# Attention on one Trainium2 core: the product of the second weight block with V written as seven smaller products in every inner period, and two partial outputs added by the Pool engine

## The chip, the cores and the metric

The kernel runs on one core of one Trainium2 chip. The metric is the device time of one execution in microseconds (us). The core has a matrix engine (TensorE; PE in the profile, its weight loads PEld), a vector engine (DVE), a scalar engine (ACT), the Pool engine (POOL) and a queue engine (SP) that only issues transfers. Each engine takes its instructions strictly in the order in which they were written, and an instruction that waits holds all that stand behind it on its engine.

## The reference

```python
# q, k, v: (8, 2048, 512) float32
d_k = q.shape[-1]
scores = np.matmul(q, k.transpose(0, 2, 1)) / np.sqrt(d_k)
attn_weights = special.softmax(scores, axis=-1).astype(np.float32)
return np.matmul(attn_weights, v)
```

## The kernel before

Both matrix products of attention are computed by Winograd's form of Strassen's method: the two operands are cut into 2 x 2 blocks, and seven block products replace eight, at the price of sums of blocks. Operands are fp16, and products gather in fp32 banks of PSUM, the memory that TensorE writes. Softmax needs no maximum here: `exp` of the scaled scores is taken at once, and the row sums come out of the second product through a column of ones that stands beside V; outputs are multiplied by their reciprocal (`rate`, L469).

**Periods and slots.** There are 8 batches, and each is cut into four periods of 28 slots: 32 periods, numbered g = 0 to 31; a period's place in its batch is g % 4, called qt. One slot holds one product of Q and K for the scores that are needed two periods later (`Group.product`, two matmuls of 512 columns at L332) and, between them, the products of weights and V that a text places there ("a6@20" is product 6 of the row block a at slot 20). Lists of words of the same form (`SUMS`, one for each qt, with some in `SUMS_AT` for single g) say at which slot which sum of blocks is given to DVE. So the order of each engine is written out by hand, and the engines run free within it, held by semaphores alone.

**Weights times V.** A period computes two row blocks, a and b, each as seven products with 256 columns (`Pair.product`, L437: eight matmuls for each product, as the contraction runs over eight pieces, `NJ`). The sums of weight blocks come from `p_sums` (L385 to L388; words S, N, L), those of V blocks from `v_sums` (L222 to L225; words v01 to v14). The weights of a pair of periods lie in the tiles `left` (two of them) and `right`.

**Inner products.** In the periods g = 1 to 29 some of these seven products are taken for a and b together and are again written as seven smaller ones of 128 columns (`fine`, L586: four matmuls each, so 28 instead of 16). Its stages 1 to 4 are the words s1..s4 for product 1 (called x), t1..t4 for product 2 (y) and u1..u4 for product 5 (z). Which of them are inner is said by `INNERS`, by qt: `("xz", "xyz", "xyz", "xz")`. So in qt 0 and 3 product 2 is still the plain one (words a2 and b2). An inner product needs four sums of weight blocks on DVE (`a_sums`, L555 to L558; words x1..x4, y1..y4, z1..z4, written to the tiles `si1`, `si2`, `si4` and in place), and once in a batch four sums of V blocks (`vi_sums`, L256 to L259; words X, Y, Z). Between its stages ACT copies a 256-column half of a bank (L601) and two 128-column parts into `ci` (L604, L609), and DVE adds the latter to a bank (L610, L614).

**Outputs.** ACT multiplies a bank of 256 columns by the reciprocal row sum into an output tile `o` (`scaled`, L446), and DVE adds a second bank to it (`final`, L449). The output quarter C11 is the sum of product 1 and product 2. Where product 2 is inner, C11 is made by `scaled` from x and `final` from y (`after2`). Where it is not, ACT copies x to a fresh bank (L529), product 2 gathers on top of it, and `scaled` writes the sum. There are seven `o` tiles. SP stores each of them (`store`, L456, 128 KB).

**Loads.** POOL issues the loads of the next batch (`load`, L127, for Q and K into two `stage` tiles; `load_v`, L214, for V), SP issues the transposing transfers from `stage` (`dma_transpose`, L153) between its stores. A load waits for the transposing transfer that empties its `stage` tile; the transposing transfer waits for the load.

Of the kernel before, what the change touches and what calls it, by code (L numbers as in the profile page):

```python
# [12 lines left out]
def kernel(  # L13
# [47 lines left out]
    NP = B * NQT  # L61
    inv_sqrt_d = float(1.0 / np.sqrt(D))
# [5 lines left out]
    opool = ctx.enter_context(tc.tile_pool(name="opool", bufs=7))  # L68
# [35 lines left out]
    si = {n: const.tile([P, NI, P], F16, name=f"si{n}") for n in (1, 2, 4)}  # L104
    ui = {n: const.tile([P, NI, P + 2 if n == 1 else P], F16, name=f"ui{n}") for n in (1, 2, 4)}
    ti3 = const.tile([P, NI, P], F16, name="ti3")
# [109 lines left out]
    def v_sums(b, c):  # L216
        vh = vraw[b % 2]
        js = slice(c * NI, (c + 1) * NI)
# [14 lines left out]
    def t3_inner(b, s):  # L233
        if s == 1:
            return ti3[:]
        if b + 1 == B:
            return vi_blocks(b + 1)[s // 2][:, 0]
        return vu_blocks()[1] if s else vi_blocks(b)[1][:, 0]
# [5 lines left out]
    def vi_sums(b, s):  # L244
        if not ti:
            for n in (1, 2, 4):
                ti[n] = ipool.tile([P, 2, NI, P + 2 if n == 1 else P], F16, tag=f"t{n}", name=f"ti{n}")
            nc.gpsimd.memset(ti[1][:, 1, :, P:P + 1], 0.0)
        if s == 2:
            b11, b12, b21, b22 = vu_blocks()  # L250
            t1, t2, t4 = ui[1][:, :, 0:P], ui[2][:], ui[4][:]
        else:
# [9 lines left out]
    def new_p(sp):  # L262
        left = [ppool.tile([P, NJ, QH], F16, tag=f"left{s}", name=f"left{s}") for s in range(2)]
        right = ppool.tile([P, NJ, 2, QH], F16, tag="right", name="right")
        pts[sp] = (left, right)
# [4 lines left out]
    def plain_tile(kb, half, name):  # L270
# [8 lines left out]
        left, right = pts[0]  # L279
# [20 lines left out]
    class Group:  # L300
# [6 lines left out]
        def product(self, n):  # L307
# [6 lines left out]
            if n == 1:  # L314
                if self.sp not in pts:
                    new_p(self.sp)
                self.left, self.right = pts[self.sp]
# [52 lines left out]
    def p_sums(g, which, j0=0, j1=NJ):  # L370

        left, right = pts[g // 2]
# [27 lines left out]
    class Pair:  # L400
# [8 lines left out]
        def product(self, n, j0=0, j1=NJ):  # L409
            g = self.g  # L410
            left, right = pts[g // 2]
# [41 lines left out]
        def store(self, o, half, ds):  # L453
            b, sp = divmod(self.g // 2, NSP)
            n = (2 * sp + half) * NT + self.g % 2 * 2 + "ab".index(self.which)
            nc.sync.dma_start(out=out[b, n * P:(n + 1) * P, ds], in_=o)  # L456
# [43 lines left out]

    class Fine(Pair):
# [18 lines left out]
        def part(self):  # L520
# [6 lines left out]
            else:  # L527
                self.y = bank("pz")
                nc.scalar.copy(out=self.y[:, 0:H], in_=self.x[:, 0:H])  # L529

        def after2(self):
            if "y" in INNER(self.g):
# [19 lines left out]
    def a_sums(g, s):  # L552
        a11, a12, a21, a22 = a_blocks(g, s)
        return [
            lambda: add(si[1][:], a21, a22),  # L555
            lambda: sub(si[2][:], si[1][:], a11),
            lambda: sub(a21, a11, a21),
            lambda: sub(si[4][:], a12, si[2][:]),  # L558
        ]

    def fine(g, s, stage):
# [8 lines left out]
        else:  # L570
            b11, _, b21, b22 = (x[:, s] for x in vi_blocks(g // NQT))
            t1, t2, t4 = ti[1][:, s, :, 0:P + s], ti[2][:, s], ti[4][:, s]
        pa, pb = (pairs.setdefault((g, w), Fine(g, w)) for w in "ab")
        name = "xyz"[s]
        if stage == 1:
            for p in (pa, pb):
                setattr(p, name, bank("pz" if s else "px"))
        xa, xb = getattr(pa, name), getattr(pb, name)

        def product(n, dst):  # L580
            lhs, rhs = {
                1: (a11, b11), 2: (a12, b21), 3: (si[4], b22), 4: (a22, t4),
                5: (si[1], t1), 6: (si[2], t2), 7: (a21, t3_inner(g // NQT, s)),
# [14 lines left out]
        if stage == 1:  # L598
# [3 lines left out]
        elif stage == 2:  # L602
            product(6, xb[:, 0:P])
            nc.scalar.copy(out=ci[:, 0], in_=xb[:, 0:P])  # L604
            product(2, xa[:, 0:P])
        elif stage == 3:
            product(3, xa[:, P:P + W])
            product(7, xb[:, 0:P])
            nc.scalar.copy(out=ci[:, 1], in_=xb[:, 0:P])  # L609
            nc.vector.tensor_add(xa[:, P:H], xa[:, P:H], ci[:, 0])  # L610
            done(pa)
        else:
            product(4, xb[:, 0:P])
            nc.vector.tensor_add(xb[:, P:H], xb[:, P:H], ci[:, 1])  # L614
# [15 lines left out]
    def INNER(g):  # L630
        return "" if g == 0 or g >= NP - 2 else "xyz" if g % NQT in (1, 2) else "xz"

    INNERS = ("xz", "xyz", "xyz", "xz")

    def INNER(g):
        return "" if g == 0 or g >= NP - 2 else INNERS[g % NQT]

    def placed(text):
# [8 lines left out]
        "a7'@1 b7'@2 a4'@6 u1@8 b4'@9 u2@9 s1@12 u3@12 s2@13 u4@14 s3@15 a3@15 s4@16 b3@18 a6@20 "  # L647
        "a2@22 b6@24 b2@27",
        "a7'@1 b7'@3 a4'@5 u1@7 b4'@10 u2@10 s1@11 u3@12 s2@13 u4@14 s3@15 a3@16 s4@17 b3@18 "
        "a6@20 t1@21 t2@23 b6@24 t3@25 t4@27",  # L650
# [286 lines left out]
```

## Time and profile before

| | |
|---|---|
| median of three timed runs | 791.18 us (790.97 to 791.58) |
| the profiled execution, its own time | 792.15 us |
| its span, from the first instruction to the last | 790.4 us |
| PE busy in the span | 783.1 us, 99% |
| DVE busy | 690.1 us, 87% |
| ACT busy | 629.1 us, 80% |
| POOL busy | 71.8 us, 9% |
| granted TensorE clock | 0.999 of full speed |

The busy time of PE says that a matmul was under way, not that PE was at its peak: matmuls are pipelined, and one that lasts 273 ns starts 109 ns after the one ahead of it. On DVE and ACT too an instruction may begin before the one ahead of it has ended. POOL's busy time before is that of issuing loads, and of a few small instructions at the start.

### The profile page before, as it was taken

Reading aid. Unit: us, or ns where it says so; the run is one execution under the profiler, and the core shown is the slowest. Engines: PE = TensorE matmul, PEld = TensorE weight load, DVE = VectorE, ACT = ScalarE, POOL = GpSimd, SP = SyncE. Lnnn points to the kernel's source line nnn. Section 1 sums busy time; section 2 is a strip of 40 time slices with the busy share of each in tenths; the row PEclk is TensorE's granted clock in tenths of the full one; section 3 lists DMA queues with packets and bytes.
Section 4 is the critical chain, followed back from the end, with each engine's and each line's share of the span. In section 5 each row is a group of like instructions: output and inputs, shape, how many; then the busy total and the mean of one; then the engine's idle time right before and its main releaser. Section 6 shows DMA issues by size and latency. Waiting matters only on the chain.

```text
span 790.4 us, 17347 instructions
## 1 busy us (share of the span) xinstructions
PE 783.1 (99%) x6406; PEld 536.7 (68%) x6406; DVE 690.1 (87%) x1508; ACT 629.1 (80%) x1267; POOL 71.8 (9%) x108
## 2 busy tenths in 40 slices
PE   8999999999999999999999999999999999999998
PEld 5556666666666666666666676666676666666686
DVE  2789999979998899988999889997999979999774
ACT  4777888887888888888888888888888888888852
POOL 4011110101100110001100101001010011000000
PEclk9999999999999999999999999999999999999999
DMA  9989996899949999398994899768897799921122
GB/s 224 179 130 159 177 186 124 142 179 153 183 104 172 176 178 185 71 170 138 189 183 98 164 166 176 146 129 156 157 171 150 133 161 163 185 68 37 45 67 96
DMA packets 206453, 116.02 MB, mean 147 GB/s; under 512 B 124320, under 2 KB 205344, under 8 KB 206368
## 3 DMA queue, kind: packets, MB, share of 16 engines
q0 software_dynamic: 49648, 49.29, 43.2%
q1 hardware_dynamic: 156432, 65.30, 38.1%
q8 instruction: 50, 0.82, 0.4%
q14 instruction: 35, 0.29, 0.1%
q10 hardware_dynamic: 288, 0.33, 0.1%
HBM read 100.73 MB, written 33.55 MB: 170 GB/s over the span
## 4 chain that ended last, share of the span: by engine, by line
PE 98%; DMA 1%; ACT 1%; DVE 0%; SPq 0%; issue 0%; ACTq 0%
PE t L332 46%; PE t L437 33%; PE t L586 15%; PE t L275 2%; DMA first<-in_k_dram 1%; PE tr L163 1%; PE t L291 0%; PE tr L140 0%; ACT left L268 0%; ACT right L268 0%; SPq L134 0%; DVE kraw L166 0%; DVE cz L357 0%; ACT cz L348 0%; ACT kraw L142 0%
## 5 line engine op out<-in xcount | busy, mean ns | idle before, releaser
L332 PE MATMUL t<-qraw,kraw 128*128 128x512 f16 x728 | 200.7, 379 | 0.1
L446 ACT ACTIVATE o<-t,r 128x256 f32<-128x256 f32 x256 | 118.5, 477 | 69.1 <-PE t L437 34.6
L268 ACT ACTIVATE left<-t 128x512 f16<-128x512 f32 (+1 forms) x260 | 154.4, 599 | 17.8 <-PE t L332 10.0
L332 PE MATMUL t<-qs,ks 128*128 128x512 f16 x488 | 139.7, 378 | 0.2 <-DVE cz L357 0.2
L268 ACT ACTIVATE right<-cz 128x1024 f16<-128x1024 f32 x122 | 129.4, 1061 | 4.5 <-DVE cz L354 4.5
L437 PEld LDWEIGHTS <-s 128*128 128x128 f16 x1072 | 103.9, 97 | 38.3 <-DVE s L388 1.7
L437 PEld LDWEIGHTS <-right 128*128 128x128 f16 x1024 | 100.1, 98 | 36.8
L332 PEld LDWEIGHTS <-kraw 128*128 128x128 f16 x976 | 88.4, 97 | 54.0 <-issue 0.6
L357 DVE TENSOR_TENSOR cz<-t,cz 128x512 f32<-128x512 f32 x122 | 83.7, 686 | 25.3 <-ACT cz L351 13.0
L348 ACT COPY cz<-t 128x512 f32<-128x512 f32 x120 | 70.4, 586 | 42.0 <-PE t L332 39.3
L354 DVE TENSOR_TENSOR cz<-t,cz 128x512 f32<-128x512 f32 x122 | 83.5, 684 | 13.4 <-PE t L332 12.7
L449 DVE SCALAR_TENSOR_TENSOR o<-t,r,o 128x256 f32<-128x256 f32 x164 | 78.1, 480 | 16.8 <-PE t L437 9.0
L332 PEld LDWEIGHTS <-ks 128*128 128x128 f16 x732 | 67.3, 97 | 34.2 <-issue 0.5
L586 PEld LDWEIGHTS <-si 128*128 128x128 f16 x876 | 62.7, 97 | 26.7 <-issue 0.2
L343 ACT COPY t<-t 128x512 f32<-128x512 f32 x120 | 69.2, 577 | 4.6 <-PE t L332 1.2
L437 PE MATMUL t<-vt,s 128*128 128x256 f16 (+1 forms) x560 | 72.5, 273 | 0.0
L332 PE MATMUL t<-qs,kraw 128*128 128x512 f16 x244 | 72.5, 379 | 0.0
L332 PE MATMUL t<-qraw,ks 128*128 128x512 f16 x244 | 72.5, 379 | 0.0
L351 ACT COPY cz<-t 128x512 f32<-128x512 f32 x122 | 70.7, 579 | 0.0
L437 PE MATMUL t<-vh,s 128*128 128x257 f16 x512 | 66.9, 272 | 0.0
L437 PE MATMUL t<-vt,right 128*128 128x256 f16 x512 | 66.2, 273 | 0.0
L437 PE MATMUL t<-vh,right 128*128 128x256 f16 x512 | 66.0, 273 | 0.0
(102 smaller groups left out, 1116.0 us busy)
## 6 DMA issues: line engine op xcount, KB each, us to landing
out_dram<-o SPq DMA_DIRECT2D x256, 128.0 KB, 2.4
vh<-in_v_dram POOLq DMA_DIRECT2D x32, 512.0 KB, 9.6
stage<-in_q_dram POOLq DMA_DIRECT2D x28, 512.0 KB, 6.7
stage<-in_k_dram POOLq DMA_DIRECT2D x28, 512.0 KB, 6.8
right<-in_q_dram POOLq DMA_DIRECT2D x2, 512.0 KB, 10.8
right<-in_k_dram POOLq DMA_DIRECT2D x2, 512.0 KB, 12.6
first<-in_q_dram SPq DMA_DIRECT2D x2, 256.0 KB, 3.5
cz<-in_q_dram SPq DMA_DIRECT2D x2, 256.0 KB, 6.8
```

The source lines that it names most:

```text
L268: nc.scalar.activation(out=out_, in_=in_, func=EXP, scale=inv_sqrt_d)
L275: nc.tensor.matmul(st[:], kops[c][0][:, n, dc, :], qraw[0][:, half * NT:(half + 1) * NT, dc, :], start=(dc == 0), stop=(dc == ND - 1),)
L332: nc.tensor.matmul(dst[:], lhs[:, j, dc, :], rhs[:, :, dc, :], start=(n in (1, 5) and dc == 0), stop=(dc == 1), skip_group_check=True,)
L343: f(out=self.y[:], in_=self.x[:])
L348: f(out=self.cz[:, 1, :], in_=self.z[:])
L351: nc.scalar.copy(out=self.cz[:, 0, :], in_=self.x[:])
L354: nc.vector.tensor_add(self.cz[:, 1, :], self.x[:], self.cz[:, 1, :])
L357: nc.vector.tensor_add(self.cz[:, 0, :], self.z[:], self.cz[:, 0, :])
L437: nc.tensor.matmul(dst[:, 0:width], lhs(j), rhs(j), start=(first and j == 0), stop=(j == NJ - 1), skip_group_check=True,)
L446: nc.scalar.activation(out=out_, in_=src, func=COPY, scale=r[:])
L449: nc.vector.scalar_tensor_tensor(out=out_, in0=src, scalar=r[:], in1=out_, op0=MULT, op1=ADD)
L586: nc.tensor.matmul(dst, lhs[:, j, :], rhs[:, j, :], start=(n == 1 and j == 0), stop=(j == NI - 1), skip_group_check=True,)
```

## The change

Product 2 becomes inner in all periods from g = 1 to 29 (`INNERS` is "xyz" for all four qt). In the 14 periods of qt 0 and qt 3 this puts the words t1..t4 in the place of a2 and b2, and the sums y1..y4 on DVE. The V sums of y (words Y1..Y4) stand in qt 0 instead of qt 1, and the third of them is written over a block of V instead of into the tile `ti3`, which goes. Where y is inner, C11 is put together in another way: `scaled` writes the part of x to one `o` tile and the part of y to another (`more`), and POOL adds the second to the first in SBUF, the memory of the other engines. There are eight `o` tiles. The two `left` tiles become one with two halves, and all lists of slots are new. Periods 30 and 31 keep their order, and the new names `END_INNERS`, `home`, `scratch`, `FULL`, `NS2` and the branches for s == 3 change nothing there as they are set.

```diff
+    INNERS = ("xyz", "xyz", "xyz", "xyz")
+    END_INNERS = {NP - 2: "", NP - 1: ""}
+    ALL = True
-    opool = ctx.enter_context(tc.tile_pool(name="opool", bufs=7))
+    opool = ctx.enter_context(tc.tile_pool(name="opool", bufs=8))
...
     def t3_inner(b, s):
-        if s == 1:
+        if s == 1 and not ALL:
             return ti3[:]
         if b + 1 == B:
-            return vi_blocks(b + 1)[s // 2][:, 0]
-        return vu_blocks()[1] if s else vi_blocks(b)[1][:, 0]
+            return (vi_blocks(b + 1)[0][:, 0], vi_blocks(b + 1)[0][:, 1], vi_blocks(b + 1)[1][:, 0], vi_blocks(b + 1)[0])[s]
+        return (vi_blocks(b)[1][:, 0], vi_blocks(b)[1][:, 1], vu_blocks()[1], vi_blocks(b)[1])[s]
...
-        left = [ppool.tile([P, NJ, QH], F16, tag=f"left{s}", name=f"left{s}") for s in range(2)]
+        left = ppool.tile([P, 2, NJ, QH], F16, tag="left", name="left")
...
         def after2(self):
+            if "y" in INNER(self.g) and self.g < NP - 2:
+                more = self.half()
+                self.scaled(more, self.y[:, 0:H], self.r1)
+                nc.gpsimd.tensor_add(self.o11, self.o11, more)
+                self.store(self.o11, 0, slice(0, H))
+                return
             if "y" in INNER(self.g):
                 self.final(self.o11, self.y[:, 0:H], self.r1)
...
-    INNERS = ("xz", "xyz", "xyz", "xz")
-
     def INNER(g):
-        return "" if g == 0 or g >= NP - 2 else INNERS[g % NQT]
+        return INNERS[g % NQT] if 0 < g < NP - 2 else END_INNERS.get(g, "")
...
     PRODUCTS = (
-        "a7'@1 b7'@2 a4'@6 u1@8 b4'@9 u2@9 s1@12 u3@12 s2@13 u4@14 s3@15 a3@15 s4@16 b3@18 a6@20 "
-        "a2@22 b6@24 b2@27",
+        "a7'@1 b7'@2 a4'@6 u1@7 b4'@9 u2@9 s1@10 u3@12 s2@13 u4@14 s3@15 a3@15 s4@17 b3@17 a6@19 "
+        "t1@20 t2@22 b6@23 t3@25 t4@27",
...
     SUMS = (
-        "v02@0 q3@1 Z3@1 L1@3 z1@4 S2@6 q4@6 z2@7 z4@7 x1@9 z3@10 x3@10 x2@11 v12@11 x4@13 S4@14 "
-        "v03@16 v13@16 N1@16 L3@16 N3@23 v04@24",
+        "v02@1 q3@1 Z3@1 L1@3 Y1@3 z1@3 S2@5 q4@6 z2@6 z4@9 x1@9 z3@10 v12@10 x3@11 x2@11 x4@13 "
+        "S4@14 Y2@16 N1@16 y1@17 v03@18 y2@18 y3@18 v04@19 y4@20 v13@22 Y3@22 Y4@23 N3@24 L3@27",
...
-        "v14@0 z1@1 S2@1 z2@3 z4@3 S4@6 Y1@7 z3@8 x1@11 x2@11 x3@12 x4@13 k01@15 y1@16 k03@17 "
-        "k04@17 y2@17 y3@18 k02@19 y4@20 Y2@20 N1@21 Y4@22 Y3@23 N3@24 q1@25 q2@27",
+        "v14@0 z1@0 S2@1 z2@3 z4@4 S4@7 z3@10 x1@11 x2@11 k01@11 x3@13 x4@13 k03@14 y1@17 k04@18 "
+        "y2@18 k02@18 y3@19 y4@20 N1@21 N3@24 q1@25 q2@27",
...
-        "z1@0 z2@0 S2@2 z4@2 k31@5 S4@6 z3@7 k33@8 x1@9 x2@11 x3@12 x4@13 X1@13 v01@15 k32@16 "
-        "k34@16 X2@17 X3@17 Z1@17 v11@18 X4@20 Z2@21 Z4@23 N1@23 q1@24 N3@24 q2@27",
+        "z1@0 k31@1 S2@2 z2@3 S4@7 k33@8 x1@8 z4@9 z3@10 k34@10 x2@11 x3@11 x4@13 X1@13 X2@14 "
+        "v01@15 v11@16 y1@17 Z1@17 X3@17 y3@17 k32@18 y2@18 N1@19 X4@21 y4@23 q1@23 Z2@24 N3@24 "
+        "Z4@25 q2@25",
...
     SUMS_AT = {
...
         1: (
-            "Z1@0 z1@0 z2@1 S2@2 Z2@2 Z3@2 Z4@3 S4@5 z3@8 x1@9 z4@11 S3@11 x2@11 x3@12 x4@13 k01@15 "
-            "y1@16 k03@17 k04@17 y2@17 y3@18 Y1@18 k02@18 y4@20 Y2@20 N1@21 Y4@22 Y3@24 N3@24 q1@25 "
+            "z1@0 Z1@1 z2@1 Z2@1 Z3@2 S2@3 z4@5 Z4@5 x1@7 S3@9 z3@9 S4@9 x2@11 x3@13 x4@13 k01@15 "
+            "k03@15 y1@16 y3@17 k04@18 y2@18 Y1@18 y4@18 k02@18 Y2@20 N1@21 Y4@21 Y3@22 N3@24 q1@27 "
             "q2@27"
```

137 lines of the change are left out of this document (88 added, 49 removed), and 4 rows, old and new, of the table SUMS.

## The prediction

> **What bounds the kernel now.** I read the chain of waits first, then the busy time of each engine in the four periods of one batch in the steady part (periods 8 to 11; a period starts where its first L332 matmul does), then the timeline of PE, then the waits.
>
> ```profile
> PE 98%; DMA 1%; ACT 1%; DVE 0%; SPq 0%; issue 0%; ACTq 0%
> ```
>
> ```profile
> 231.18:255.18 24.00, 24.00 (x193) 16.41 (x192) 21.82 (x44) 20.34 (x41) 2.22 (x3) 1.00 0.88 152
> 255.18:278.99 23.81, 23.81 (x206) 16.43 (x204) 19.85 (x47) 19.70 (x42) 2.22 (x3) 1.00 1.02 173
> 278.99:302.81 23.82, 23.82 (x207) 16.41 (x205) 23.05 (x53) 19.79 (x42) 3.70 (x5) 1.00 1.00 175
> 302.81:326.80 23.99, 23.99 (x195) 16.40 (x193) 22.29 (x52) 19.83 (x40) 0.74 (x1) 1.00 0.60 121
> ```
>
> The columns are the stretch, its length, then busy us and instructions of PE, PEld, DVE, ACT and POOL, the granted clock, the DMA share, GB/s. PE fills each period, and the waits of PE between 100 and 740 us are an empty list: no other engine sets the steady part. Yet DVE is at 97% in the third period, and only 1.7 us of waiting of weight loads on it shows in the whole run (on the sums of L388, seven times). So what the change saves of TensorE's own work is the gain to be had, and DVE the cover that may give way. The first and last row are the periods with the plain product 2 (192 matmuls; the x counts include strays at the edges), the middle ones those with the inner y (204).
>
> ```profile
> 299.98 1.04 PE L437 MATMUL t<-vt,s 128*128 128x256 f16 x8
> 301.28 0.39 PE L586 MATMUL t<-vh,si 128*128 128x128 f16 x4
> ```
>
> Eight wide matmuls end 1.04 us after the first starts; one lasts 273 ns (its group's mean), so they start (1.04 - 0.273)/7 = 0.110 us apart. Four narrow ones, of 219 ns: (0.39 - 0.219)/3 = 0.057.
>
> Only the start of the steady part is not clean:
>
> ```profile
> 63.30:87.74 24.44, 24.23 (x207) 16.47 (x205) 23.98 (x55) 19.64 (x42) 2.96 (x4) 1.00 1.00 167
> 87.74:111.56 23.82, 23.82 (x208) 16.43 (x205) 22.94 (x53) 19.76 (x42) 3.70 (x5) 1.00 1.00 166
> ```
>
> Period 1 has the same matmuls as period 2 and takes 0.62 us more, with DVE busy in 23.98 of 24.44 us: there DVE is the bound.
>
> **The change, part by part.** *TensorE.* In each of the 14 periods, 16 wide matmuls go and 28 narrow ones come: 16 x 0.110 = 1.75 us against 28 x 0.057 = 1.60, so 0.16 by rounded rows. The whole periods give it more exactly: 24.00 - 23.82 = 0.18 and 23.99 - 23.81 = 0.18. 14 x 0.18 = **2.55 us** off the path.
>
> *DVE.* These rows price what is added (last numbers: busy in all, mean ns):
>
> ```profile
> L556 DVE TENSOR_TENSOR si<-si,left 128x512 f16<-128x512 f16 x44 | 18.5, 421 | 5.2 <-PE t L586 4.2
> L614 DVE TENSOR_TENSOR t<-t,ci 128x128 f32<-128x128 f32 x73 | 21.4, 293 | 2.0 <-ACT o L446 1.8
> L449 DVE SCALAR_TENSOR_TENSOR o<-t,r,o 128x256 f32<-128x256 f32 x164 | 78.1, 480 | 16.8 <-PE t L437 9.0 <-ACT o L446 3.6 <-issue 1.7
> ```
>
> A newly inner period gains four y sums (4 x 0.42) and two adds (2 x 0.29): 2.26 us. qt 0 also takes the four Y sums (1.67) from qt 1; qt 1 and qt 2 lose two finals each (0.96); one L sum (0.42) moves from qt 0 to qt 1 and one from qt 2 to qt 3. By these durations qt 0 comes to 21.82 + 2.26 + 1.67 - 0.42 = 25.3 us, qt 1 to 17.6, qt 2 to 21.7, qt 3 to 22.29 + 2.26 + 0.42 = 25.0, in periods of 23.82: two over-full by 1.2 and 1.5. But ops that follow directly overlap: a 128x512 sum at 242.76 us is 0.41 long, and the next starts 0.32 later. At the pace of direct followers in the timeline (0.33 for such a sum, 0.20 for an add to a bank, 0.40 for a final, 0.60 for 128x1024 and the cz adds, 1.13 for 128x2048, 0.08 for a reciprocal) the lists come to 22.6, 18.8, 20.6 and 23.0 us after, and to 19.9, 19.4, 21.7 and 22.1 before. Busy time lies 0.2 to 1.9 above that before, from ops that begin after a wait and overlap nothing; a fuller queue has fewer. So qt 3 and qt 0 are full with 0.8 and 1.2 us to spare by the one count, short by 1.2 and 1.5 by the other. I take the pace, as full queues run by it, and cost the DVE work at nothing: it is covered by that room, by slots of the lists (y1 stands three slots, 2.5 us, ahead of t1), and by the 5 us of qt 1 behind the two full periods. Without the cover it is the 2.7 us of the durations a batch, less what the sums have in hand; R2 prices it.
>
> *ACT.* Newly inner: two `scaled` (2 x 0.477), two copies to `ci` (0.27 each), one of L601 (0.40), less two of L529 (0.36 each): +1.18 us, so 20.34 becomes 21.5. The others gain two `scaled`: 20.7. At most 90% of 23.82; at nothing.
>
> *Pool.* Two adds of 128x256 a period, 58 in all. No row shows one. POOL's nearest rows read one operand:
>
> ```profile
> L775 POOL CAST ident<-ident 128x128 f16<-128x128 f32 x1 | 0.3, 293 | 2.5 <-DMA ident<-attn_identity 2.5
> L828 POOL CAST gate<-qraw 128x1 f32<-128x1 f16 x1 | 0.2, 183 | 23.3 <-DMA qraw<-right 23.3
> ```
>
> (293 - 183)/127 = 0.87 ns an element. 256 elements at one operand's pace: 0.41 us; at half of it: 0.63. I take 0.6; off the path, since an add's `o` tile is wanted again nine slots (7.6 us) later at the earliest in the built order. What it may do to DVE is a rival.
>
> *Queues.* The adds stand on POOL at the end of each period, ahead of loads that it used to issue up to a period early (two Q loads of the next batch now come after them, at the start of qt 0). Their transposing transfers stand at slots 10 and 12, and the loads take 6.7 us (8 slots) to land: at nothing, with two slots to spare. On SP the C11 stores now wait for POOL. The extra `o` tile, the merged `left` and the new `si` shape add no instruction: 10 `o` tiles a period of eight, the shortest reuse of a stored tile 11 slots (9.4 us) against 2.4 us of a store.
>
> *Period 1.* Two finals (2 x 0.40 at their overlapped pace) leave the DVE queue that bounds it: between 0 and the whole 0.62 us back; I take 0.5, as 0.8 leaves.
>
> **Sum.** 792.15 (the profiled execution: span 790.4 and 1.75 around it) - 2.55 - 0.5 = 789.1. That execution lies 0.97 above the median of 791.18, so **788.1 us** for the median.
>
> **The rivals.** About 0.2% (1.6 us) can be told from no change: 789.6 to 792.8.
>
> *R1: POOL's adds hold up some DVE sums.* Add and sum read two operands from SBUF at once, which no row of this trace shows. If one or two of the four adds of the two full periods keep a sum waiting for half of their 0.6 us: 0.3 to 0.6 us a batch, 2.1 to 4.2 in all: 790.2 to 792.3. For it: DVE is nearly always busy there. Against: over a third of DVE's time has an operand in PSUM (the cz and bank adds, the finals). The Trainium skill (SBUF — State Buffer, "Who interferes with whom") says that a DVE instruction with two SBUF inputs and a Pool instruction reading SBUF exclude each other, the second one waiting for the whole of the first; by that rule R1 or R2 is the outcome. No run shown here bears on it. Its GPSIMD Engine Reference ("Elementwise — side-by-side cycle accounting") has 4497 ns for a 2048-element add; an eighth is an estimate of 0.56 us, within my bounds.
>
> *R2, slower: DVE becomes the bound in qt 0.* The place is the sum s4 of slot 14, which product 3 of slot 15 needs, and the y sums behind it. It decides once DVE is held over 3.05/7 = 0.44 us a batch beyond its room. Price: both adds met in full (2 x 0.63) and the 0.5 us by which it may outlast its room: 1.1 to 1.8 us a batch, 788.1 + 7.7 to 12.6 = 795.8 to 800.7; partly met, from 792.8. For: the count by durations. Against: the third period ran at 97% busy without a wait of PE.
>
> *R3, slower: SP.* The store of b's C11 waits for POOL, and behind it is the transposing transfer of the next batch's first K chunk:
>
> ```profile
> 256.31 3.20 SPq L153 DMA_TRANSPOSE kraw<-stage  x1
> ```
>
> POOL's wait for it ended near 261.5, 5.2 us on. Its first reader on DVE moves from slot 16 to slot 11, near 264.5. An add and a store put ahead shift it by 1.0 to 1.7 us: it still lands 1.3 us early. If not, DVE stands, about a slot: 7 x 0.85 = 6 us, 794.
>
> *R4: the narrow matmuls don't save* because of 12 more weight loads. The periods with inner y already carry them at 23.82 us, so hardly: 791.2.
>
> **Numbers.** Forecast 0.50; R1 0.22; R2 0.15; R3 0.08; R4 and the rest 0.05. Faster: the forecast and the low edge of R1, 0.54. Same: the most of R1 and R4, 0.22. Slower: R2, R3 and an edge, 0.24. The forecast's own range is 787.4 to 789.1: period 1 gives its 0.62 back whole or not at all, 14 x 0.01 from the rounding of the 0.18, and 0.4 for the spread of the runs. As both signs hold much of the chance, the range for all reaches on over R1, R4 and the lowest part of R2 to 793.5; what it leaves out, R3 and the rest of R2, is 2 in 10.
>
> **What would show it.** Right: steady periods all at 23.8 us, no waits of PE after 100 us, DVE busy about 94%. R1 and R2: sums of 128x512 or 128x2048 longer than 0.42 or 1.22 us beside POOL's adds, weight loads waiting on the s sums, qt 0 above 24 us. R3: DVE waiting for kraw. Period 1 at 24.4 again would take 0.5 back. A Pool add over 1 us would make the forecast wrong.

## The result, and the profile after

The changed kernel takes **794.36 us** (median of six runs, 793.93 to 794.9), the kernel before 791.48 us beside it (six runs, 790.97 to 791.74): a ratio of 1.0037, interval 1.0024 to 1.005. It is 2.9 us slower, where 3.1 us of gain had been forecast. Its lines in the profile have other numbers: L332 is now L342 (Q and K), L437 is L447 (plain products of weights and V), L586 is L634 (inner products), L449 is L459 (`final`), and the Pool add is L555.

The chain of waits of the changed kernel, first its shares by engine:

```profile
PE 96%; DVE 2%; ACT 1%; issue 1%; DVEq 0%; ACTq 0%
```

DVE is on the chain now, where it had 0% before. Periods 8 to 11 (qt 0, 1, 2, 3), in the columns of the prediction's table:

```profile
230.51:254.70 24.19, 24.19 (x207) 16.36 (x205) 24.09 (x54) 20.72 (x44) 5.63 (x7) 1.00 0.94 166
254.70:278.61 23.91, 23.91 (x208) 16.42 (x205) 20.27 (x46) 20.17 (x43) 4.04 (x5) 1.00 1.13 191
278.61:302.43 23.82, 23.82 (x208) 16.44 (x205) 22.27 (x50) 21.04 (x45) 5.11 (x7) 1.00 1.01 177
302.43:326.60 24.17, 24.06 (x207) 16.36 (x205) 23.66 (x55) 20.10 (x42) 1.38 (x2) 1.00 0.35 84
```

All four hold the same matmuls, and 23.82 us is what these take. So qt 0 loses 0.37 us, qt 1 0.09 and qt 3 0.35, and in the first and the last of them DVE is busy for 24.09 of 24.19 and 23.66 of 24.17 us. The clock is 1.00 throughout. Which weight loads wait, between 100 and 740 us (total, times, longest):

```profile
PEld L447 <- DVE right L397: 2.7, 7, 0.4
...
PEld L634 <- DVE si L589: 1.3, 7, 0.2
...
PEld L634 <- DVE si L588: 1.2, 7, 0.2
```

Seven each, one a batch: the first in qt 3 (product a7' at slot 1), the others in qt 0 (slots 9 and 10). (An ellipsis in a fence or a code cut stands for lines left out.) Why DVE is late shows in the groups of the same profile: the Pool add, three kinds of DVE sum, and one that adds to a bank (count, busy in all and mean ns):

```profile
L555 POOL TENSOR_TENSOR o<-o 128x256 f32<-128x256 f32 x58 | 51.1, 882 | 307.9 <-ACT o L456 221.2 <-issue 82.9 <-DMA out_dram<-o 3.4
...
L213 DVE TENSOR_TENSOR qraw<-qraw 128x1024 f16<-128x1024 f16 x15 | 16.0, 1067 | 0.0
L588 DVE TENSOR_TENSOR si<-s 128x512 f16<-128x512 f16 x29 | 15.8, 545 | 0.2
L231 DVE TENSOR_TENSOR vt<-vh,vt 128x1024 f16<-128x1024 f16 x16 | 13.4, 835 | 0.0
...
L364 DVE TENSOR_TENSOR cz<-t,cz 128x512 f32<-128x512 f32 x122 | 83.5, 684 | 4.0 <-PE t L342 3.6
```

The sums of 128x1024 and 128x512 lasted 0.68 and 0.42 us before; here their means are 1.07, 0.84 and 0.55. L364, which reads a bank, keeps its 0.684. The start of qt 0 in the timeline shows one case, DVE and POOL side by side (start, us):

```profile
328.28 0.68 DVE L229 TENSOR_TENSOR vt<-vh,vt 128x1024 f16<-128x1024 f16 x1
328.88 1.22 DVE L213 TENSOR_TENSOR qraw<-qraw 128x1024 f16<-128x1024 f16 x1
```

```profile
327.55 2.00 POOL L555 TENSOR_TENSOR o<-o 128x256 f32<-128x256 f32 x2 [21.86 <-ACT o L456]
```

Alone an add takes 0.72 us (the shortest of the 58). The second of these two began at 328.3, with L229; it took 1.20 us, and L213 behind L229 took 1.22, 0.54 beyond its own 0.68. Add and sum had waited for one another.

To put a number on it for each run, I took every DVE instruction that lasted over 0.06 us longer than the median of its operation and shape in that run, and added up what it lasted beyond: **16.6 us** in the changed kernel (42 sums, up to 0.54 us each), nothing in the kernel before. No instruction with an operand in PSUM is among them. The second measure is the time of periods 1 to 28, from the first L342 matmul of one to that of the next: 670.02 us before, 673.08 after. The times in the table below are medians of the runs in the faster of two states; only e9 had slow ones, two of six at 809.9 us.

### The profile page after: what moved, and what is told of

Its sections match the earlier page's. It is cut to its first block, busy times and chain, and to the rows that moved or that the text cites. A ratio compares the mean times of both kernels' runs of the same rounds, so it can differ in the third digit from the quotient of the medians.

```text
span 792.4 us, 17987 instructions
## 1 busy us (share of the span) xinstructions
PE 786.1 (99%) x6574; PEld 536.6 (68%) x6574; DVE 712.4 (90%) x1562; ACT 646.3 (82%) x1339; POOL 124.1 (16%) x166
## 4 chain that ended last, share of the span: by engine, by line
PE 96%; DVE 2%; ACT 1%; issue 1%; DVEq 0%; ACTq 0%
PE t L342 45%; PE t L447 29%; PE t L634 17%; PE t L285 2%; DVE cz L367 1%; DVE ks L196 1%; PE tr L169 1%; PE tr L146 0%; PE t L853 0%; PE t L301 0%; DVE right L397 0%; ACT right L278 0%; ACT o L456 0%; ACT left L278 0%; DVE s L396 0%
## 5 line engine op out<-in xcount | busy, mean ns | idle before, releaser
L456 ACT ACTIVATE o<-t,r 128x256 f32<-128x256 f32 x314 | 143.9, 480 | 88.0 <-DVE r L482 33.2
L342 PE MATMUL t<-qraw,kraw 128*128 128x512 f16 x728 | 198.0, 379 | 0.1
L342 PE MATMUL t<-qs,ks 128*128 128x512 f16 x488 | 138.7, 379 | 0.1
L342 PEld LDWEIGHTS <-kraw 128*128 128x128 f16 x976 | 87.1, 97 | 57.9 <-issue 0.6
L447 PEld LDWEIGHTS <-right 128*128 128x128 f16 x1024 | 99.5, 98 | 38.3 <-DVE right L397 2.7
L447 PEld LDWEIGHTS <-s 128*128 128x128 f16 x1072 | 102.1, 97 | 30.5 <-issue 0.3
L634 PEld LDWEIGHTS <-si 128*128 128x128 f16 x1044 | 75.4, 97 | 39.4 <-issue 1.4
L555 POOL TENSOR_TENSOR o<-o 128x256 f32<-128x256 f32 x58 | 51.1, 882 | 307.9 <-ACT o L456 221.2
L342 PEld LDWEIGHTS <-ks 128*128 128x128 f16 x732 | 67.9, 97 | 40.2 <-issue 0.2
L364 DVE TENSOR_TENSOR cz<-t,cz 128x512 f32<-128x512 f32 x122 | 83.5, 684 | 4.0 <-PE t L342 3.6
L634 PEld LDWEIGHTS <-left 128*128 128x128 f16 x928 | 66.2, 97 | 20.6
L459 DVE SCALAR_TENSOR_TENSOR o<-t,r,o 128x256 f32<-128x256 f32 x134 | 62.5, 478 | 19.0 <-ACT ci L652 6.4
L447 PE MATMUL t<-vt,s 128*128 128x256 f16 (+1 forms) x560 | 72.5, 273 | 0.0
L342 PE MATMUL t<-qs,kraw 128*128 128x512 f16 x244 | 72.5, 378 | 0.0
L342 PE MATMUL t<-qraw,ks 128*128 128x512 f16 x244 | 72.4, 378 | 0.0
L634 PE MATMUL t<-vh,left 128*128 128x128 f16 x696 | 67.3, 219 | 0.0
```

Source lines behind the costliest of these rows:

```text
L342: nc.tensor.matmul(dst[:], lhs[:, j, dc, :], rhs[:, :, dc, :], start=(n in (1, 5) and dc == 0), stop=(dc == 1), skip_group_check=True,)
L364: nc.vector.tensor_add(self.cz[:, 1, :], self.x[:], self.cz[:, 1, :])
L447: nc.tensor.matmul(dst[:, 0:width], lhs(j), rhs(j), start=(first and j == 0), stop=(j == NJ - 1), skip_group_check=True,)
L456: nc.scalar.activation(out=out_, in_=src, func=COPY, scale=r[:])
L459: nc.vector.scalar_tensor_tensor(out=out_, in0=src, scalar=r[:], in1=out_, op0=MULT, op1=ADD)
L555: nc.gpsimd.tensor_add(self.o11, self.o11, more)
```

## The experiments

The theory under test (**theory 1**): a Pool add and a DVE sum with both operands in SBUF exclude each other, and in qt 3 and qt 0, where DVE is full, what the sums wait reaches TensorE. Its main rival (**theory 2**): DVE is over-full there from the y sums alone. In the texts below "a batch" is four periods.

| run | median us | ratio to before, interval | stretched, us | periods 1 to 28, us |
|---|---|---|---|---|
| changed kernel | 794.36 | 1.0037, 1.0024 to 1.005 | 16.6 | 673.08 |
| e1 no add | 788.59 | 0.9963, 0.9951 to 0.9976 | 0 | 667.13 |
| e2 write only | 789.06 | 0.9975, 0.9967 to 0.9984 | 0 | 667.83 |
| e5 Pool copy | 789.18 | 0.9982, 0.9967 to 0.9997 | 1.4 | 667.87 |
| e3 DVE finals | 798.18 | 1.0088, 1.0074 to 1.0102 | 0 | 676.47 |
| e12 late adds only | 792.50 | 1.0012, 1.0003 to 1.002 | 7.6 | 671.33 |
| e4 before, with Pool adds | 798.24 | 1.0105, 1.0079 to 1.0131 | 6.3 | 676.80 |
| e8 DMA add in SBUF | 819.83 | 1.0361, 1.034 to 1.0383 | 0 | 696.09 |
| e9 DMA add in DRAM | 798.00 | 1.0089, 1.0067 to 1.0111 | 0 | 677.06 |
| e14 DMA add, store held | 799.28 | 1.0106, 1.0082 to 1.0131 | 0 | 678.99 |
| e10 Pool and DMA | 792.72 | 1.002, 1.0012 to 1.0029 | 9.5 | 670.81 |
| e15 finals and DMA | 792.73 | 1.0024, 1.0015 to 1.0033 | 0 | 675.96 |
| e13 later adds | 794.33 | 1.0047, 1.0028 to 1.0066 | 14.0 | 673.06 |
| e16 placed adds | 790.04 | 0.9988, 0.9978 to 0.9997 | 7.5 | 671.51 |
| e17 placed, store held | 790.15 | 0.9989, 0.998 to 0.9998 | 8.9 | 669.25 |
| e18 placed by fills | 788.67 | 0.997, 0.9958 to 0.9982 | 7.4 | 667.78 |

The last two columns are of one profiled execution each. Those of e15 and e16 (797.92 and 792.4 us) lie far above the medians of their runs, with one long period 22 of 28.48 and 26.33 us; their medians stand for them.

### Is it the add? e1, e2, e5, e3

e1 takes one line out of the changed kernel; e2 and e5 put something else in its place:

```diff
-                nc.gpsimd.tensor_add(self.o11, self.o11, more)
```

```diff
+                nc.gpsimd.memset(more, 0.0)
```

```diff
+                nc.gpsimd.tensor_copy(out=self.o11, in_=more)
```

> The Pool add is left out, and with it the second part of C11 in the inner periods; all else is the changed kernel (ACT still scales both parts, the stores stay). Theory 1 (a Pool add and a VectorE sum with both operands in SBUF exclude each other; about 2.0 us of stretched sums a batch make the 0.82 us of TensorE stall a batch): no sum is stretched any more (the 128x512 sums at 0.41-0.42 us, the 128x1024 ones at 0.68-0.69), periods 3 and 0 of a batch fall from 24.17 and 24.19 us to 23.8-23.9, and the time to 788.0-789.3 us. Theory 2 (VectorE is over-full in periods 3 and 0 with the sums of y alone, the adds do not matter): the stalls stay, 793-794.5 us.

> In the place of each Pool add, POOL fills the tile of the second part with zeros: it writes 128x256 fp32 and reads nothing; the second part of C11 is left out. Theory 1 in its narrow form (what excludes is that POOL reads SBUF): like the run without adds, within 0.4 us, 788.0-789.5 us, sums not stretched. Theory 1 in a wide form (any Pool work in SBUF beside a sum): the sums stay stretched, to the length of the fill, and the time lies between 790 and 794.5 us. Theory 2: 793-794.5 us.

> Each Pool add becomes a Pool copy of the second part over the first: one operand read from SBUF and not two; the first part of C11 is lost. Theory 1 (reading SBUF is what excludes, for the length of the instruction): sums are stretched here too, by less as the copy is shorter than the add (between the fill's 0.31 us and the add's 0.72 us): 40 to 100% of the changed kernel's loss of 5.8 us against the run without adds, 790.9-794.4 us. Rival (only a Pool instruction with two operands excludes, or none but the length counts and the copy is as short as the fill): 788.6-789.4 us, as with the fill (789.06 us).

Without the adds TensorE has no stall left, and no weight load waits on DVE between 100 and 740 us. The same periods of e1, qt 0 and qt 3:

```profile
228.56:252.41 23.85, 23.85 (x208) 16.44 (x205) 23.61 (x54) 20.61 (x44) 2.22 (x3) 1.00 0.85 160
...
300.04:323.86 23.82, 23.82 (x207) 16.38 (x205) 23.10 (x56) 20.08 (x42) 0.74 (x1) 1.00 0.62 122
```

DVE has 23.61 us of work in 23.85 and keeps up: theory 2 is out. Theory 1's ranges for e1 and e2 held. For e2 and e5 the POOL groups:

```profile
L555 POOL MEMSET o<- 128x256 f32 x58 | 18.1, 311 | 331.5 <-ACT o L456 311.5 <-POOL o L555 11.1 <-issue 8.9
```

```profile
L555 POOL COPY o<-o 128x256 f32<-128x256 f32 x58 | 31.7, 546 | 320.5 <-ACT o L456 230.7 <-issue 89.8
...
L213 DVE TENSOR_TENSOR qraw<-qraw 128x1024 f16<-128x1024 f16 x15 | 11.6, 774 | 0.0
```

The fill writes as many bytes as the add and takes 0.31 us each time; it neither waits nor makes a sum wait. The copy takes 0.40 us alone and 0.55 on the mean, so it does wait; of the sums only L213 behind L229 is longer, seven times by 0.20 us, in the very place where the add cost 0.54. So it is reading that excludes, and one operand read holds a sum for less than half of what two do. Here **my expectation of e5 missed**: I had reckoned the loss in proportion to the copy's length (40 to 100%), and it was 0.6 of 5.8 us.

By the periods even that little is not what the held sums cost. e2, which holds up no sum, has 667.83 us for periods 1 to 28 and e5 667.87, against 667.13 in e1; both lose the 0.70 us at slots 13 and 14 of qt 3, 0.06 us in six batches and 0.34 in one. One output of ACT in qt 3, in e1 and then in e2, shows where it begins:

```profile
308.51 0.47 ACT L456 ACTIVATE o<-t,r 128x256 f32<-128x256 f32 x1 [0.29 <-PE t L447]
```

```profile
309.56 0.47 ACT L456 ACTIVATE o<-t,r 128x256 f32<-128x256 f32 x1 [0.35 <-PE t L447]
```

The `o` tile that it writes was last used by POOL, so in e2 ACT waits for POOL too. By the trace this is one more wait instruction, after which the output starts 0.06 us later (0.34 in period 7), and ACT's copies up to slot 14 are late by as much. The changed kernel loses the same 0.70 us at the same slots. So of its 5.95 us over e1, 5.25 are left for held sums.

In the prediction R1 named a rule of the Trainium skill for this (SBUF — State Buffer, "Who interferes with whom"): two-operand DVE instructions contend with Pool instructions that read SBUF, and not with ones that only write it. The traces agree in both halves: 1.22 for 0.68 us beside the add, and 0.31 us fills with no sum stretched. In the prediction the second one waits for the whole of the first; here a sum waited for at most 0.54 us of an add of 0.72, and for 0.20 of a copy of 0.40.

e3 gives C11 back to DVE in all inner periods:

```diff
-            if "y" in INNER(self.g) and self.g < NP - 2:
-                more = self.half()
-                self.scaled(more, self.y[:, 0:H], self.r1)
-                nc.gpsimd.tensor_add(self.o11, self.o11, more)
-                self.store(self.o11, 0, slice(0, H))
-                return
             if "y" in INNER(self.g):
                 self.final(self.o11, self.y[:, 0:H], self.r1)
```

> The seven smaller products stay in all inner periods, and both parts of C11 are joined by VectorE as in the kernel before (one operand in PSUM, 0.40-0.48 us each). Theory 1: no stretched sums (-2.0 us of VectorE a batch), eight finals more (+3.2 us a batch): VectorE has 1.2 us a batch more to do than in the changed kernel, half of it in the two full periods, so 793-798 us, slower than the changed kernel or equal to it. If the Pool adds cost more than the stretch that the trace shows (a wait elsewhere that they cause), it is faster than the changed kernel: 791-793.5 us. Theory 2: VectorE alone sets the stall, so 3.2 us more a batch show in the two full periods at 0.8 us each: about 10 us more, 800-805 us.

798.18 us: more by 3.8 us than with Pool adds, just above the top of theory 1's range and below theory 2's. Its qt 0 took 24.58 us, with DVE busy for 24.38 of them. So POOL was the better place for the work of the two, and neither is free.

### Where does it hurt? e12, e4

```diff
+                if self.g % NQT >= 2:
                     nc.gpsimd.tensor_add(self.o11, self.o11, more)
```

> Pool adds after periods 2 and 3 alone (they fall into periods 3 and 0); after periods 0 and 1 the add is left out, and with it the second part of C11 there. Theory 1 with its place (only what falls into VectorE's two full periods costs): periods 3 and 0 at 24.1-24.2 us as in the changed kernel, 1 and 2 at 23.82, 793.2-794.4 us. Rival (58 adds at some 0.1 us each, wherever they run): 30 adds, 788.6 + 3.0 = 791.6 us.

792.50 us, between the two: with the 28 adds that fall into qt 3 and qt 0 alone, 4.2 of the 5.95 us are there that all 58 cost in periods 1 to 28; the rest comes with the other 30, and 0.8 us of it is lost in qt 1 and qt 2 themselves. So "only the full periods" was too narrow, and "the same price for each add" (2.9 us for 28; the text above reckons with 30) too low for these.

e4 puts the Pool add into the kernel before, with its own lists and its seven `o` tiles:

```diff
-            self.final(self.o11, self.y[:, 0:H], self.r1)
+            more = self.half()
+            self.scaled(more, self.y[:, 0:H], self.r1)
+            nc.gpsimd.tensor_add(self.o11, self.o11, more)
```

> The kernel before (seven smaller products for C11 in periods 1 and 2 alone, its own order of sums), with the Pool adds in the place of VectorE's finals there. Theory 1: sums beside the adds are stretched here too (0.42 to 0.75 us, 0.68 to 1.02-1.22 us), but VectorE has 1.7 us and more to spare in these periods, and loses 1.6 us of finals a batch: no stall, 790.6-791.8 us. Rival (an add costs TensorE time wherever it runs, some 0.1 us each as in the changed kernel, where 58 of them came with about 5.8 us): 28 adds cost 2.8 us, 793.5-794.5 us.

798.24 us, and neither theory's figure: the loss has another cause. Nearly all of it, 0.45 to 1.33 us seven times, is lost at slot 2 of qt 3, where TensorE waits for a copy of ACT. Its waits of ACT between 100 and 740 us have a line that neither kernel has:

```profile
ACT o L446 <- DMA out_dram<-o: 10.9, 5, 2.8
```

With `more` a period takes ten `o` tiles from a ring of seven, and ACT stands until a store has left one (1.9 to 2.8 us ahead of that copy in all seven; each time ACT goes on some 0.08 us after a store has landed); TensorE waits for ACT's copies behind that. Whether these adds would be free with an eighth tile, which the changed kernel has, was not tried.

### Can the add be taken off both engines? e8, e9, e10, e14, e15

e8 lets a DMA that POOL issues add the second part to the first in SBUF; e9 lets it add to the stored first part in DRAM:

```diff
+                nc.gpsimd.dma_start(out=self.o11, in_=more, accum_op=ADD)
                 self.store(self.o11, 0, slice(0, H))
```

```diff
                 self.store(self.o11, 0, slice(0, H))
+                nc.gpsimd.dma_start(out=self.rows(0, slice(0, H)), in_=more, accum_op=ADD)
```

> Each Pool add becomes a DMA that POOL issues and that adds the second part onto the first in SBUF (128 KB each); the sum is complete. Theory 1: no instruction of POOL reads SBUF beside the sums, so none is stretched and periods 3 and 0 fall to 23.8-23.9 us; the store of C11 then waits some 2-3 us for the DMA and holds up what is behind it on SP: 788.2-790.5 us if nothing of that is due soon, up to 794 if the K transposition behind it comes late. Theory 2: 793-794.5 us.

> Each Pool add becomes a DMA that POOL issues and that adds the second part onto the stored first part in the output in DRAM; SP stores the first part at once and waits for no DMA, the sum is complete. Theory 1: no sum is stretched, as without adds (788.59 us), and SP's K transpositions are no longer behind a store that waits for a DMA, as they were with the DMA into SBUF (819.83 us, its periods 1 of a batch at 26.2-31.9 us): all inner periods at 23.8-23.9 us, 788.4-789.6 us. Rival (the DMAs themselves cost, not the wait on SP): period 1 stays long and the time is 800 us or more; in between, 790-796 us, if POOL's wait of about 2.5 us for each store to land makes a load behind it late.

No sum is stretched in either, and in e8 qt 2, qt 3 and qt 0 stand at 23.81 to 23.90 us. But qt 1 took up to 31.89. Of e8, period 9, and then the 4.0 us in it behind a gap of TensorE:

```profile
255.10:286.99 31.89, 25.92 (x207) 17.52 (x205) 19.61 (x46) 20.34 (x43) 4.85 (x6) 0.89 1.02 172
```

```profile
274.10:278.10 4.00, 4.00 (x23) 2.92 (x24) 2.33 (x9) 1.97 (x5) 0.74 (x1) 0.50 1.01 148
```

SP's queue in e8 at the start of that period (255 to 285 us):

```profile
SPq L469 <- DMA o<-o: 11.3, 2, 10.9
```

The store of C11 waited 10.9 us for the adding DMA, and behind it on SP stood the transposition of the next batch's first K chunk; a K sum of DVE waited 7.8 us for that chunk, and TensorE 6 us for what stood behind the sum. So R3 of the prediction is real as a mechanism, and dearer than priced there. In e9 POOL waits for each store to land, its loads come late, and DVE waits 15.8 us in all for K; 798.0 us lies in none of the ranges, above the one given for late loads.

e14 is e8 with the two stores of qt 0 issued at slot 9 of qt 1, behind the second K transposition:

```diff
+                if self.g % NQT:
+                    self.store(self.o11, 0, slice(0, H))
+                else:
+                    held.append(self)
...
+        if (qt, slot) == (1, 9):
+            while held:
+                p = held.pop(0)
+                p.store(p.o11, 0, slice(0, H))
```

> The sum is complete, by DMA adds into SBUF after every inner period; the two stores of C11 of period 0 are issued on SP behind the transposition of the second K chunk (slot 9 of period 1) and no longer ahead of that of the first. Theory 1 (neither place of a Pool add is free, in periods 3 and 0 nor in period 1; the DMA add takes nothing from VectorE, and its only cost was SP's wait ahead of the K transposition): all inner periods at 23.8-23.9 us, 788.4-789.8 us. Rival (the DMA adds are late or slow in themselves, or their traffic delays the loads): period 1 above 24.3 us, 792 us or more.

799.28 us: the rival. Now SP waits 34.2 us in all for K *loads* to land, a wait that e1 does not have; the median K load takes 8.4 us instead of 6.9. Whether that comes of the adding DMAs ahead of it in POOL's queue or of their traffic was not told apart. A DMA add is free for DVE, not for the loads.

e10 uses Pool adds after qt 0 and qt 1 and DMA adds after qt 2 and qt 3; e15 uses DVE's finals after qt 0 and DMA adds elsewhere, with one sum of qt 1 moved:

```diff
+                if self.g % NQT < 2:
+                    nc.gpsimd.tensor_add(self.o11, self.o11, more)
+                else:
+                    nc.gpsimd.dma_start(out=self.o11, in_=more, accum_op=ADD)
```

```diff
-            if "y" in INNER(self.g) and self.g < NP - 2:
+            if "y" in INNER(self.g) and self.g % NQT and self.g < NP - 2:
...
-        "v14@0 z1@0 S2@1 z2@3 z4@4 S4@7 z3@10
+        "v14@0 S2@1 z1@2 z2@3 z4@4 S4@7 z3@10
```

> The sum is complete: after periods 0 and 1 of a batch the Pool add of the changed kernel, whose time falls into periods 1 and 2, where VectorE has 1.5 us and more to spare; after periods 2 and 3 the DMA add into SBUF of the earlier run, whose periods 3 and 0 ran at 23.82-23.85 us and whose long periods were all of number 1, behind the adds of period 0. Theory 1: all inner periods at 23.8-23.95 us, 788.4-789.8 us, faster than both kernels. Rival (a DMA add costs wherever it stands, by SP's wait): 795 us or more. Rival (each Pool add costs TensorE some 0.1 us wherever it runs): 28 adds, 791.4 us.

> The sum is complete: after periods 1, 2 and 3 of a batch the DMA add into SBUF (periods 2, 3 and 0 ran at 23.81-23.85 us behind it in both runs that had it there); after period 0, behind which neither a Pool add nor a DMA add was free, VectorE's two finals, and in period 1 one sum of z (0.34 us at VectorE's pace) issued behind the finals of the period before and no longer ahead of them. With finals after every period, period 1 stood at 24.10 us, 0.28 us over; the moved sum should take that away. Theory 1: all inner periods at 23.8-23.95 us, 788.5-790.0 us, faster than both kernels; with the 0.28 us left, 790.6 us. Rival (the DMA adds delay the K chunks of the next batch wherever they run): periods above 24.3 us, 792 us or more.

Both missed theory 1's range, at 792.7 us. In e10 qt 0 and qt 3 are clean, and qt 2 but for two periods, but qt 1 took 23.9 to 24.9 us. The start of one, DVE and POOL:

```profile
254.50 1.32 DVE L231 TENSOR_TENSOR vt<-vh,vt 128x1024 f16<-128x1024 f16 x1
255.74 0.94 DVE L591 TENSOR_TENSOR si<-s 128x512 f16<-128x512 f16 x1
```

```profile
254.52 1.88 POOL L556 TENSOR_TENSOR o<-o 128x256 f32<-128x256 f32 x2
```

Two adds back to back hold up two sums by 0.64 and 0.52 us, just ahead of the `cz` sum and the finals that TensorE needs at slots 4 and 6. So the 3.6 us that DVE has to spare in that period as a whole did not help. Such places carry 1.6 of the 3.2 us that e10 loses in qt 1; the other 1.5 are lost at slot 15 in three batches, where DVE had waited 1.5 to 2.1 us for the K chunk: R3 again. In e15 qt 1 loses 0.41 us at slot 11 in all six batches, with DVE's `cz` sum late, and in three of them 0.2 to 1.3 more at slot 15, after waits of 1.5 to 2.6 us for K; whether the moved sum did the first stays open. With that e15 lies in its rival's range, that the DMA adds delay the K chunks.

### Does the place of an add decide? e13, e16, e17, e18

If an add costs what DVE is running at that moment, moving it by a microsecond must change its price. These kernels keep all 58 adds and delay some of them: POOL first copies one column of `more` (so that it waits for ACT), then fills a small tile `pad` several times (0.18 us each, and fills hold up nothing, by e2).

```diff
+    pad = const.tile([P, 96], F32, name="pad")
...
+                pause = {(2, "a"): 12, (2, "b"): 9, (3, "b"): 8}.get((self.g % NQT, self.which), 0)
+                if pause:
+                    nc.gpsimd.tensor_copy(out=pad[:, 0:1], in_=more[:, 0:1])
+                for _ in range(pause):
+                    nc.gpsimd.memset(pad[:], 0.0)
                 nc.gpsimd.tensor_add(self.o11, self.o11, more)
```

> All 58 Pool adds stay and the sum is complete; the adds after period 2 and the second one after period 3 start later by 1.2-1.8 us, so that each should read beside a VectorE operation with an operand in PSUM (a 0.68 us sum of Group, or a final). POOL is kept busy for that time by a copy of one column and 8 to 12 fills of 128x96, and fills stretched no sum in their own run. Theory 1 (place decides): fewer stretched sums in periods 3 and 0, stalls of 0.1-0.4 us a batch in the place of 0.82, 789.0-791.4 us; where the delay misses its operation by 0.3 us, less of that. Rival (the number of adds decides, not their place): 793.8-795 us.

The time, 794.33 us, is the rival's. The periods say more: qt 3 is at 23.83 us in all batches, so there the delay took the whole stall away. In qt 0 the add came 1 us too late and hit another sum (24.19 us in four of seven batches). And qt 1, with 0.09 us lost in the changed kernel, now loses 0.1 to 1.0. Of these 4.3 us in six batches 2.0 are lost at slot 15, where DVE had waited 1.5 to 2.0 us for K (R3), and the rest mostly at slots 3 and 6, behind held sums. One of them, and the two adds beside it:

```profile
255.27 2.24 DVE L232 TENSOR_TENSOR vt<-vh,vt 128x1024 f16<-128x1024 f16 x1
```

```profile
255.52 1.42 POOL L561 TENSOR_TENSOR o<-o 128x256 f32<-128x256 f32 x2
```

A sum of 0.68 us waited for both adds. That left open whether a stall can be removed at all or only moves on. e16 places five of the eight adds of a batch by the timelines of earlier runs, each to begin in the sum ahead of an operation that reads a bank:

```diff
-                pause = {(2, "a"): 12, (2, "b"): 9, (3, "b"): 8}.get((self.g % NQT, self.which), 0)
-                if pause:
+                pause = {
+                    (0, "a"): 1, (0, "b"): 0, (2, "a"): 12, (2, "b"): 9, (3, "b"): 3,
+                }.get((self.g % NQT, self.which), -1)
+                if pause >= 0:
```

> As the run with later adds (all 58 Pool adds, sum complete), with three changes of place: the second add after period 3 starts 1.1 us earlier than there (3 fills for 8), to read beside the two finals; of the two adds after period 0 the first starts behind a copy of one column and one fill, to read beside a 0.68 us sum of Group, and the second behind such a copy, to read beside the two finals. Adds after period 2 stay where they stopped the stall of period 3. Theory 1 (an add costs by what VectorE runs at that moment, and not by itself): the stalls of 0.36 us in period 0 and of 0.1 to 1.0 us in period 1 go or fall to 0.1, 788.6-790.6 us, faster than both kernels. Rival (an add that does not hold up one sum holds up another of the same length, so the stall only moves on): stretched sums stay near 12-14 us in all and the time at 792.5-794.5 us.

**790.04 us**, within theory 1's range and the first complete kernel under the kernel before. qt 0 and qt 3 are clean; qt 1 still loses 0.3 to 0.7 us in three batches, at slot 15, behind a K chunk: the store of C11, later by the pause, again stands ahead of the K transposition on SP. e17 issues these stores behind it, as e14 did, but at slot 1 of qt 1:

```diff
+        if (qt, slot) == (1, 1):
+            while held:
```

> As the run with placed adds (sum complete), but SP stores C11 of period 0 behind the transposition of the next batch's first K chunk and no longer ahead of it. With the stores ahead, that transposition was issued some 2 us after the start of period 13, and 0.2 us before it in the run without adds; a K sum of VectorE waited 2.1 us for the chunk, and TensorE 0.58 us. Theory 1 with the queue of SP as the last step (R3 of the prediction, small and in some batches): period 1 at 23.82-23.9 us in all batches, VectorE not waiting for K, 788.6-789.8 us. Rival (POOL's own delays make the loads late): period 1 stays at 24.1-24.5 us in some batches, 789.7-790.4 us, as with the stores ahead.

Period 1 of a batch is at 23.82 us in all seven, and DVE waits for K only once, 0.5 us: that part was R3. But the time is the rival's, 790.15 us, as qt 0 lost 0.37 us in five batches. e16 and e17 differ there by a race on POOL: the copied column gets in ahead of a DVE sum, or behind it. Start of period 12 at 325.10 us in e17:

```profile
327.61 1.06 POOL L563 TENSOR_TENSOR o<-o 128x256 f32<-128x256 f32 x1
```

```profile
328.01 0.95 DVE L269 TENSOR_TENSOR vt<-vt 128x512 f16<-128x512 f16 x1
328.88 0.86 DVE L460 SCALAR_TENSOR_TENSOR o<-t,r,o 128x256 f32<-128x256 f32 x2
```

The add started 2.51 us into the period, met L214, waited for its end and then held L269 for 0.53 us. In e16 it started at 3.08 us, inside L269, and read beside the two finals; no sum was held. e18 drops the column for this add and uses six fills, which wait for nothing:

```diff
-                    (0, "a"): 1, (0, "b"): 0, (2, "a"): 12, (2, "b"): 9, (3, "b"): 3,
+                    (0, "a"): 1, (0, "b"): 0, (2, "a"): 12, (2, "b"): 9, (3, "b"): 6,
...
-                if pause >= 0:
+                if pause >= 0 and self.g % NQT < 3:
```

> As the run with placed adds and held stores (sum complete), but the second add after period 3 is delayed by 6 fills alone, with no copy of a column ahead, which in that run came now before and now behind a 128x1024 sum of VectorE: the add then started 2.51 us (5 batches, period 0 at 24.22 us) or 3.07 us (2 batches, 23.85 us) after the period's start. With fills alone it starts near 2.95 us in every batch, in the 128x512 sum ahead of the two finals. Theory 1 (place decides, to some tenths of a us): period 0 at 23.85 us in all batches, all inner periods clean, 788.3-789.5 us. Rival (the rest lies in the pauses themselves): 789.8-790.5 us.

**788.67 us** (six runs, 788.09 to 789.59), ratio 0.997, interval 0.9958 to 0.9982: 0.3% faster than the kernel before, and within 0.1 us of the run without any add. POOL and DVE in e18, the same place (period 12 starts at 325.03):

```profile
327.88 1.03 POOL L563 TENSOR_TENSOR o<-o 128x256 f32<-128x256 f32 x1
```

```profile
327.90 0.42 DVE L269 TENSOR_TENSOR vt<-vt 128x512 f16<-128x512 f16 x1
328.24 0.87 DVE L460 SCALAR_TENSOR_TENSOR o<-t,r,o 128x256 f32<-128x256 f32 x2
```

The add waits for L269 (1.03 us for its own 0.72), and DVE for nothing. qt 0 stands at 23.85 us in all batches, and 7.4 us of stretched sums remain elsewhere. TensorE loses 0.65 us over e1 (667.78 against 667.13): 0.2 in period 2, and 0.4 in period 25, behind a late K chunk. e12, with sums held for 7.6 us, lost 4.2. So where a held sum lies matters more than how long sums are held in all.

## Why the prediction was wrong

**The step that failed** is the line on the Pool: "I take 0.6; off the path, since an add's `o` tile is wanted again nine slots (7.6 us) later at the earliest". I looked for who waits for the add's *result*, and nobody does; what waits is the sum that reads SBUF at the same time. With it fell the DVE step, "I take the pace ... and cost the DVE work at nothing": for sums that nothing holds up it was right (e1 has no stall, with DVE busy for 88.25 of the 95.30 us of a batch), though with less room than counted: DVE is idle there for 0.24 us of qt 0, not 1.2. R1 had the mechanism, with 0.22, but one or two held sums a batch and a price of 0.3 to 0.6 us; six sums were held a batch, and it was 5.25 / 7 = 0.75.

- **TensorE, -2.55 us.** Right in kind. In e1 the periods of qt 0 and qt 3 went from 24.00 to 23.85 and 23.82: seven of each, periods 3 to 28, give 2.25. (14 x 0.18 is 2.52; the prediction has 2.55.) R4 is out.
- **Period 1, -0.5.** All 0.62 came back, 24.44 to 23.82 us in e1.
- **DVE and Pool, 0.** In their place +5.25, by held sums. With the 0.70 of ACT below, over periods 1 to 28: 670.02 - 2.25 - 0.62 + 5.25 + 0.70 = 673.10 against 673.08 measured, and 667.15 against 667.13 without the adds. The last two terms are differences between runs (changed kernel, e2, e1), so this checks the first two. The median moved by +2.88.
- **Size of an add.** Bounds 0.41 to 0.63 us; alone it takes 0.72, on the mean 0.88 with its waits. One operand's rate from two casts was too low a base. The estimate that the prediction took from the Trainium skill (GPSIMD Engine Reference, "Elementwise — side-by-side cycle accounting"), 0.56 us, was too low too.
- **R1's "against"**, that over a third of DVE's time has an operand in PSUM, is true, and is what e18 uses; but an add finds such an operation by chance. Beside the 58 adds of the changed kernel 42 sums came out longer.
- **R2** named the right period, qt 0, but its place, product 3 at slot 15, had only 0.09 us a batch; 0.26 were lost at slots 9 and 10, ahead of it. Not named was qt 3, with 0.28 at slot 1: the first add of qt 2 falls on a K sum (at 302.66 us, 0.72 us instead of 0.42) ahead of the sum that product a7' needs.
- **R3** did not happen in the changed kernel (DVE waits 0.2 us for K in all), but a later store brings it: 0.3 to 0.7 us in three batches of e16, where the K transposition left some 2 us late, and 8 us in one period of e8, where the store waited 10.9 us.
- **ACT and queues at nothing**: right for the room, as ACT was busy 20.1 to 21.0 of 23.8 us. Not reckoned with were ACT's extra waits for POOL, 0.70 us in all (e2).

The chances were set wrongly as well: R1 and R2 stood on a mechanism for which a rule was at hand, and against which I had only that DVE often reads PSUM. 0.50 for a forecast that needs 58 adds to miss each other's sums was too much.

## What to carry to other kernels

Work moved to an idle engine is priced at what it does to the engines beside it, before its own length: list for the new instruction which memory it reads, and which instructions of its neighbours read there in that stretch. The room of a busy engine counts between one due time and the next, not over a period: 3.6 us spare in a period of qt 1 of e10 did not cover two held sums ahead of slot 6. Where such work cannot be dropped, its place can be chosen, and a neighbour that is not harmed (here an operation that reads a bank) is the place; a delay made of instructions that wait for nothing held its place in e18, and one with a copy that reads SBUF beside the sums did not in e17.

## What the runs showed of the hardware

- POOL instructions that only write SBUF (58 fills of 128x256 in e2) and 58 DMA issues of 0.88 us (e8) held up no sum; a copy that reads one operand did for up to 0.20 us, an add that reads two for up to 0.54 (once, in e4, 0.77), and two adds in a row for up to 1.56.
- Both sides wait: a Pool add behind a 128x1024 sum takes 1.20 us instead of 0.72.
- One more semaphore for ACT to wait for delayed its output by 0.06 us in qt 3 of e2, though POOL's last fill had ended 6 us before.
- After the gap of 6 us in e8 TensorE's granted clock was 0.50 for the next 4.0 us of work, so the stall cost more than its length. The Trainium skill (TensorE: Matmul & The Clock Gate, "Part 1: The HAM clock gate") has it so: after idling the clock is half until about 3.4 us of sustained work. The trace agrees in kind, with 4.0 us at 0.50.
